# A shifted copy in DRAM: two free-running DMA queues, or one queue in turns with waits

## The chip, the cores and the metric

The kernel runs on one core of a Trainium2 chip. The metric is the device time of one execution in microseconds; the time of a kernel is the median over its runs. The profiles show one execution each.

## The reference

```python
def setup_inputs():
    return {"x": np.random.randn(8192, 8192).astype(np.float32)}

def reference(x):
    return np.fft.ifftshift(x)
```

For an even size in both dimensions this swaps the four quadrants: `out[r, c] = x[(r + 4096) % 8192, (c + 4096) % 8192]`. Nothing is computed; 268.44 MB are read and as many written. A half row, 4096 float32 or 16 KB, is the longest run that is contiguous in both `x` and `out`. Rows lie 32 KB apart.

## The kernel before

All work is DMA from DRAM to DRAM; SBUF isn't used. `copy(queue, row, h, step)` issues one transfer (L29) of 256 half rows, 4 MB: output rows `row` to `row + 255`, left half (`h = 0`) or right half (`h = hc`). Its access pattern has the outer dimension `[C, ENGINES]`: 16 rows that follow each other, one for each of the core's 16 DMA engines. The middle one, `[step * C, per]` with a step of 16, gives an engine 16 rows, each 16 rows on from the one before. So in a transfer the sixteen engines go side by side through adjacent rows. A half row is one packet.

The loop (L36 to L39) takes 1024 rows at a time in four blocks of 256. The sync queue (engine SP, DMA queue q1 in the profile) copies the left halves of the blocks in order, the scalar queue (ACT, q10) the right halves, two blocks off. That makes 32 transfers on each queue. The kernel writes no waits itself; the framework that orders the program adds them. At the start each queue issues four transfers; each later one waits for the transfer four before it on its queue. So up to eight transfers (32 MB) are in flight. At the end of the program (L65) SP waits for what has not landed. L54 belongs to the program's setup.

Of the kernel before, what the change touches and what calls it, by code (L numbers as in the profile page):

```python
# [1 line left out]

# [4 lines left out]


ENGINES = 16


@with_exitstack
def kernel(
    ctx: ExitStack,
    tc: tile.TileContext,
    x: bass.AP,
    out: bass.AP,
):
    nc = tc.nc
    R, C = x.shape  # L20
    hr = R // 2
    hc = C // 2
    per = 16
    rows = ENGINES * per

    def copy(queue, row, h, step):

        dims = [[C, ENGINES], [step * C, per], [1, hc]]
        queue.dma_start(  # L29
            out=bass.AP(out.tensor, out.offset + row * C + h, dims),  # L30
            in_=bass.AP(x.tensor, x.offset + (row + hr) % R * C + hc - h, dims),
        )

    for first in range(0, R, 4 * rows):  # L36
        for n in range(4):
            copy(nc.sync, first + n * rows, 0, ENGINES)
            copy(nc.scalar, first + (n + 2) % 4 * rows, hc, ENGINES)  # L39


# [1 line left out]
_INS = ['x']  # L43
_OUTS = [((8192, 8192), 'float32')]


def kernel(**inputs):
    import numpy as _np
    import concourse.bacc as _bacc
    import concourse.tile as _tile  # L50
    from concourse import mybir as _mybir
    from concourse.bass_utils import run_bass_kernel_spmd as _run

    nc = _bacc.Bacc("TRN2", target_bir_lowering=False, num_devices=1)  # L54
    arrays, args = {}, []
    for name in _INS:
        a = _np.ascontiguousarray(inputs[name])
        if a.dtype.kind in "iu":
            a = a.astype(_np.int64)
        arrays[f"in_{name}_dram"] = a  # L60
        args.append(nc.dram_tensor(f"in_{name}_dram", a.shape, _mybir.dt.from_np(a.dtype), kind="ExternalInput").ap())
    for i, (shape, dtype) in enumerate(_OUTS):
        dt = _mybir.dt.from_np(_np.dtype(dtype))
        args.append(nc.dram_tensor(f"out_{i}_dram", shape, dt, kind="ExternalOutput").ap())
    with _tile.TileContext(nc) as tc:  # L65
        kernel(tc, *args)
    r = _run(nc, [arrays], core_ids=[0])
    got = tuple(r.results[0][f"out_{i}_dram"] for i in range(len(_OUTS)))
    return got[0]
```

## Time and profile before

| | |
|---|---|
| median of 2 runs | 823.39 us (820.27 to 826.52) |
| span of the profiled execution | 812.4 us |
| recorded times less this span | 7.9 and 14.1 us, 11.0 at the median |
| data moved | 268.44 MB read, 268.44 MB written |
| share of the 16 DMA engines' span | q1 49.7%, q10 49.5% |
| transfers | 32 by SP, 32 by ACT, 4096 KB each |
| from issue to landing, median | 101.0 us |

The span is from the first to the last instruction on the core; the time of a run also holds what lies around it. The profile names a DMA queue's share as the time that its packets took, over the span of sixteen engines: shares that add up to 100% mean that no engine was without a packet. In a table of stretches each row has the stretch, its length, the busy time of GpSimd (only the setup), the granted clock, the DMA share and GB/s.

### The profile page before, as it was taken

How to read it: one execution, taken by the hardware profiler on the slowest of the kernel's cores; microseconds unless marked ns; L12 is line 12 of the kernel's file. 1: busy time of each engine (PE TensorE's matmuls, PEld its weight loads, DVE VectorE, ACT ScalarE, POOL GpSimd, SP SyncE). 2: the span in 40 equal slices, each digit the busy share in tenths (PEclk: the TensorE clock that was granted, in tenths of full speed). 3: DMA queues.
4: the chain of work that ended last, by engine and by line, in shares of the span. 5: the costliest groups of instructions: out<-in, count | busy, mean ns of one | idle time of the engine just before them, and what ended most of it. 6: DMA issues, size and time to landing. Idle time of an engine off the chain costs nothing. (4 is left out here: it accounts for less than half of the span.)

```text
span 812.4 us, 109 instructions
## 1 busy us (share of the span) xinstructions
POOL 0.2 (0%) x4
## 2 busy tenths in 40 slices
POOL 0000000000000000000000000000000000000000
DMA  9999999999999999999999999999999999999998
GB/s 307 331 331 336 335 331 331 335 325 337 334 332 336 331 333 332 334 339 332 332 334 331 329 331 334 332 328 333 330 334 335 334 328 333 332 331 330 338 331 280
DMA packets 17408, 268.44 MB, mean 330 GB/s; under 512 B 1024, under 2 KB 1024, under 8 KB 1024
## 3 DMA queue, kind: packets, MB, share of 16 engines
q1 hardware_dynamic: 8704, 134.22, 49.7%
q10 hardware_dynamic: 8704, 134.22, 49.5%
HBM read 268.44 MB, written 268.44 MB: 661 GB/s over the span
## 5 line engine op out<-in xcount | busy, mean ns | idle before, releaser
L54 POOL MEMSET const-bfloat16-1.0<- 128x1 bf16 x1 | 0.1, 101 | 0.0
L54 POOL MEMSET const-uint8-127<- 128x1 uint8 x1 | 0.1, 101 | 0.0
L54 POOL MEMSET const-float32-0.0<- 128x1 f32 x1 | 0.1, 98 | 0.2 <-issue 0.2
L54 POOL MEMSET const-float32-1.0<- 128x1 f32 x1 | 0.1, 98 | 0.0
## 6 DMA issues: line engine op xcount, KB each, us to landing
out_dram<-in_x_dram SPq DMA_DIRECT2D x32, 4096.0 KB, 101.0
out_dram<-in_x_dram ACTq DMA_DIRECT2D x32, 4096.0 KB, 101.0
```

What stands on the lines that cost most here:

```text
L54: nc = _bacc.Bacc("TRN2", target_bir_lowering=False, num_devices=1)
```

## The change

The ACT queue is no longer used. `copy` gets the number of half rows per engine and a semaphore, and its pattern is one dimension of `16 * per` rows in place of two. The 8192 rows are cut into eight parts of 1024. Each part has its own turn size (half rows per engine in a turn) and rest. A turn copies `16 * turn` rows, first all the left halves, then in a turn of its own all the right halves. Part 0 issues its eight transfers of 4 MB at once. In the other parts a turn is two transfers: the main one, of `turn - rest` half rows per engine, and behind it the rest. Before the main one SP waits until all main transfers so far have landed; rests are not waited for until the end. The block is kept in the order written, with its own two semaphores.

```diff
-    per = 16
-    rows = ENGINES * per
 
-    def copy(queue, row, h, step):
+    def copy(queue, row, h, per, sem):
 
-        dims = [[C, ENGINES], [step * C, per], [1, hc]]
+        dims = [[C, ENGINES * per], [1, hc]]
+        dst = out.offset + row * C + h
+        src = x.offset + (row + hr) % R * C + hc - h
         queue.dma_start(
-            out=bass.AP(out.tensor, out.offset + row * C + h, dims),
-            in_=bass.AP(x.tensor, x.offset + (row + hr) % R * C + hc - h, dims),
-        )
+            out=bass.AP(out.tensor, dst, dims),
+            in_=bass.AP(x.tensor, src, dims),
+        ).then_inc(sem, ENGINES)
 
+    part = 1024
+    plan = ((16, 0), (16, 1), (16, 2), (16, 3), (16, 4), (32, 2), (32, 3), (8, 2))
 
-    for first in range(0, R, 4 * rows):
-        for n in range(4):
-            copy(nc.sync, first + n * rows, 0, ENGINES)
-            copy(nc.scalar, first + (n + 2) % 4 * rows, hc, ENGINES)
+    with tc.tile_critical(), nc.semaphore("main") as main, nc.semaphore("end") as end:
+        mains = ends = 0
+        for k, (turn, rest) in enumerate(plan):
+            rows = ENGINES * turn
+            for first in range(k * part, (k + 1) * part, rows):
+                for h in (0, hc):
+                    if rest:
+                        nc.sync.wait_ge(main, mains)
+                    copy(nc.sync, first, h, turn - rest, main)
+                    mains += ENGINES
+                    if rest:
+                        copy(nc.sync, first + ENGINES * (turn - rest), h, rest, end)
+                        ends += ENGINES
+        nc.sync.wait_ge(main, mains)
+        nc.sync.wait_ge(end, ends)
```

The program before issues 32 transfers on SP and 32 on ACT; the changed one issues 120 on SP (8 in part 0, 112 in the others) and none on ACT. 56 turns begin with a wait.

## The prediction

> **What bounds the kernel now.** I read the page's head and its DMA section first: no compute engine works, and the sixteen DMA engines are full.
>
> ```profile
> span 812.4 us, 109 instructions
> ...
> DMA packets 17408, 268.44 MB, mean 330 GB/s; under 512 B 1024, under 2 KB 1024, under 8 KB 1024
> ## 3 DMA queue, kind: packets, MB, share of 16 engines
> q1 hardware_dynamic: 8704, 134.22, 49.7%
> q10 hardware_dynamic: 8704, 134.22, 49.5%
> HBM read 268.44 MB, written 268.44 MB: 661 GB/s over the span
> ```
>
> The two queues' packets (q1 is fed by SP, q10 by ACT) took 99.2% of sixteen engines' span. So the time is set by how long a packet of 16 KB, one half row, occupies an engine. 16384 of the packets carry data, 1024 for each engine.
>
> Next I read the DMA view of the middle alone, 10 to 800 us, to have a steady rate without the two ends.
>
> ```profile
> DMA packets 17017, 262.56 MB, mean 332 GB/s; under 512 B 992, under 2 KB 992, under 8 KB 992
> ```
>
> 262.56 MB in 790 us is 332.4 GB/s, or 20.8 GB/s for each engine: one half row per engine every 0.79 us. All 268.44 MB at this rate are 807.7 us.
>
> Then the stretches around the start and the end, and the waits of SP, because the change makes many small starts and ends out of one of each.
>
> ```profile
> 0.00:2.10 2.10, 0.20 (x4) 1.00 0.00 0
> 2.10:2.30 0.20, 0.00 (x0) 1.00 3.31 819
> ...
> 2.00:3.00 1.00, 0.00 (x0) 1.00 1.05 262
> 3.00:6.00 3.00, 0.00 (x0) 1.00 1.04 404
> 6.00:9.00 3.00, 0.00 (x0) 1.00 1.00 350
> 9.00:12.00 3.00, 0.00 (x0) 1.00 0.99 328
> 12.00:15.00 3.00, 0.00 (x0) 1.00 0.98 300
> ...
> 806.00:808.00 2.00, 0.00 (x0) 1.00 0.96 328
> 808.00:810.00 2.00, 0.00 (x0) 1.00 0.54 180
> 810.00:813.00 3.00, 0.00 (x0) 1.00 0.01 5
> ```
>
> The last column is GB/s, the one before it the DMA share; a packet's bytes count where it starts.
>
> ```profile
> L29 SPq DMA_DIRECT2D out_dram<-in_x_dram x32: 571/571/652, 0.7 to 708.6; - x32
> ...
> DMA to landing us min/median/max: 25.6/101.0/103.4
> ...
> SPq L29 <- DMA out_dram<-in_x_dram: 689.4, 28, 25.3
> SPq L65 <- DMA out_dram<-in_x_dram: 102.2, 2, 79.5
> ```
>
> SP issues first at 0.73 (timeline), and the first packets start at about 2.1: 1.4 us from an issue to bytes. SP's last issue ends at 708.6 + 0.57 = 709.2, and its last wait ends 102.2 us later, at 811.4: the last landing. SP does wait 28 times already (L29), but for the oldest of eight transfers in flight, with about 100 us of work queued behind it. Those waits cost no DMA time: the share is 1.00 from 20 us on.
>
> **The change, part by part.**
>
> *Same work.* The bytes, the 16 KB packets and their number per engine stay: 1024 x 0.79 us, 807.7 us in all, if the rate stays. Semaphore packets grow from 64 to 120 for each engine; the 64 of before lie inside a share of 99 to 100% and show no gap, so I cost the other 56 at nothing.
>
> *ACT's issues move to SP.* SP issues 120 transfers instead of 32. At 0.57 us that is 68 us of an otherwise waiting SP, spread over more than 800. The second issue of a turn (the rest) runs while the engines work on the first, so it is free. Only the 0.57 us of the first issue after a wait is exposed, and that is inside the 1.4 us above. A transfer of 480 rows in place of 256 may take longer to issue: between nothing and another 0.57 us; I take nothing, from the flat 571 ns of the shape seen.
>
> *The waits.* This is the term that counts. Up to part 0 there is no wait. From part 1 on each of the turns (8 each in parts 1 to 4, 4 each in parts 5 and 6, 16 in part 7) starts with a wait until every engine has landed the main share of the turn before: 56 waits. Behind the waiting instruction on SP stand the turn's main issue, its rest and all later turns; nothing else feeds the engines. So while the slowest engine ends, the semaphore travels and the new issue takes effect, the engines have only the rest of the turn before: 1 to 4 half rows each.
>
> What a wait costs with no rest at all, the one start and the one end of this profile tell together. From the first issue to the last landing are 811.4 - 0.7 = 810.7 us, at the steady rate the bytes need 807.7. So one run-down and one restart cost 3.0 us: 1.4 of the restart and 1.6 of engines that run out one after another (180 and 5 GB/s in the last rows) and of landing, less what the quick first microseconds give back. I take the 1.4 whole. The 1.6 comes after 810 us in which the engines could drift apart; after a turn of 6 to 25 us they should be closer, so I take three quarters, 1.2: 2.6 us for a bare wait. Its bounds are 3.0 (all of it) and 1.4 (no drift, landing for nothing). A rest of R covers R x 0.79 us.
>
> The cover of a wait is the rest of the turn before, so a part's first wait has the rest of the part before it. Counted from the plan: 1 wait with no rest, 8 with a rest of 1, 27 with 2, 12 with 3, 8 with 4.
> - rest 0: 2.6 x 1 = 2.6
> - rest 1: (2.6 - 0.79) x 8 = 14.5
> - rest 2: (2.6 - 1.58) x 27 = 27.5
> - rest 3: (2.6 - 2.37) x 12 = 2.8
> - rest 4: covered, 0
>
> Sum 47.4 us. With 3.0 for a bare wait it is 3.0 + 17.7 + 38.3 + 7.6 = 66.6; with 1.4 it is 1.4 + 4.9 = 6.3. If the longer issue is exposed too, 56 x 0.57 = 32 us come on top.
>
> *The layout.* Before, the sixteen engines copy sixteen adjacent rows at a time (outer dimension ENGINES, step ENGINES inside). Now one dimension of 16 x per rows is handed out; if each engine gets a run of it, engines stand 6 to 31 rows (192 to 992 KB) apart, and all work on the same half. No row shows this layout. The bounds I take are the slowest and quickest stretches of the start: 300 GB/s (12 to 15 us) and 404 (3 to 6 us). I take the steady 332, since q1 and q10 hold opposite halves and no slice of the page's middle leaves 325 to 339 whatever their mix.
>
> The Trainium skill's page "DMA: Bandwidth & Descriptors", section "Latency and other measured facts", speaks against a layout of far rows: copies between HBM tensors ran at 207 GB/s with a pitch of 512 KiB and at 214 with the pitch padded. No run here shows it yet. Taken for all parts, 807.7 x 214 / 207 would be 27 us more, an estimate from that page.
>
> *Sum.* Span 812.4 + 47.4 = 859.8 us. The two recorded times are 820.27 and 826.52, median 823.39, so 11.0 us lie around the span at the median. Forecast 870.8, say 871 us: 5.8% slower.
>
> **The rivals.**
>
> *Lockstep pays (faster).* A common start seems to run better: 404 GB/s at 3 to 6 us, 350 at 6 to 9, against 332. Each wait that lets engines idle starts them together again, and the 7/8 of the bytes in parts 1 to 7 (234.9 MB, 706.7 us) could run at the rate of a fresh start. From 2 to 9 us 2.52 MB started, 361 GB/s: 234.9 MB then take 651 us, 56 less, which with 47 of waits gives 823 - 9 = 814. At 404 throughout it is 581 us, 125 less: 745. It decides above 356 GB/s, where 234.9 MB take 47 us less; it counts as faster from 365. For it: the start is no single packet, but 6 us. Against it: 9 to 15 us ran at 328 and 300, below the mean, so the lead was given back within a turn; the first rows count sixteen packets that had only started; and rests of 3 and 4 leave no idle time in which engines could line up. "HBM Reference" of the Trainium skill, section "Specifications (TRN2)", gives about 716 GB/s for a domain, 358 each way for a copy; by it the time would not fall below 823 - 51 + 47 = 819. The trace's 661 read and written agrees; its 404 each way in three microseconds does not.
>
> *The rest hides the wait.* If engines stay within a packet of each other and landing is quick, only rests of 0 and 1 leave a gap: 6.3 us, 830 us, within 2%. For it: 1.4 us of restart is less than two packets. Against it: the end needs more than 2 us to run down.
>
> *The layout is worse.* At the 300 GB/s of the slowest stretch 268.44 MB take 895 us, 87 more: 958 with the waits. For it: nothing but the distance of the rows and the same half on all engines. Against it: the steady rate under any mix.
>
> **How the numbers follow.** My forecast has 0.5: 835 to 920 (6.3 plus some landing at the low end, 98 us of waits and longer issues at the high one). Lockstep 0.2, of which 0.15 ends more than 2% faster and 0.05 about even; the hidden wait 0.13; the worse layout 0.17, at 900 to 960. About 2% is what a measurement of this kernel can tell from no change. So faster 0.16, same 0.18, slower 0.66. The range that holds 8 in 10 leaves out the far lockstep and the far layout: 790 to 925.
>
> **What would show it.** In the profile after, the DMA share of the stretches: 1.00 in part 0 (to about 100 us), some 0.87 in part 1 (rest 1, 1.8 us of 12.6 + 1.8 idle), 0.92 in part 2, 0.98 in part 3, 1.00 in part 4, 0.96 in part 5, 0.99 in part 6 and 0.86 in part 7 (1.0 us of 6.3 + 1.0), and the mean of a busy engine unchanged, so that GB/s falls as the share. SP's waits on the copy's line should be 56 beside the last ones. I am wrong if the share falls but the GB/s does not (lockstep), if the share stays at 1.00 in part 1 (the wait is hidden), or if the GB/s in part 0, where nothing waits, is already off 332 (layout or the single queue).

## The result, and the profile after

The changed kernel takes 878.62 us (878.32 to 878.92, two runs) against 823.39 us: 1.0667 times as long, 95% interval 1.0594 to 1.0741. The forecast was 871.

The head of the page after, with its only working queue:

```profile
span 877.1 us, 168 instructions
...
DMA packets 18305, 268.45 MB, mean 306 GB/s; under 512 B 1920, under 2 KB 1920, under 8 KB 1920
...
q1 hardware_dynamic: 18304, 268.44, 92.1%
...
HBM read 268.44 MB, written 268.44 MB: 612 GB/s over the span
```

Where 99.2% of the engines' span were packets, it is 92.1% now. These 7.1% of 877 us are 62 us more than before in which engines have nothing to do.

The same by stretches, one for each part of the plan (DMA share and GB/s last):

```profile
2.00:108.00 106.00, 0.00 (x0) 1.00 0.98 317
108.00:223.00 115.00, 0.00 (x0) 1.00 0.88 292
223.00:333.00 110.00, 0.00 (x0) 1.00 0.92 305
333.00:441.00 108.00, 0.00 (x0) 1.00 0.94 308
441.00:548.00 107.00, 0.00 (x0) 1.00 0.94 313
548.00:658.00 110.00, 0.00 (x0) 1.00 0.94 309
658.00:763.00 105.00, 0.00 (x0) 1.00 0.97 318
763.00:875.00 112.00, 0.00 (x0) 1.00 0.84 302
```

Share and rate don't move alike. Part 7 has the lowest share, 0.84, and yet moves 302 GB/s, more than part 1 with 0.88 and 292. Part 0, which has no wait, has 317 and is below the 332 GB/s of before.

The start of the changed kernel, and SP's waits:

```profile
2.00:3.00 1.00, 0.00 (x0) 1.00 0.82 262
3.00:6.00 3.00, 0.00 (x0) 1.00 0.98 371
6.00:9.00 3.00, 0.00 (x0) 1.00 1.02 333
9.00:12.00 3.00, 0.00 (x0) 1.00 0.96 289
12.00:15.00 3.00, 0.00 (x0) 1.00 0.97 289
```

```profile
SPq L34 <- DMA out_dram<-in_x_dram: 766.4, 56, 71.5
SPq L56 <- DMA out_dram<-in_x_dram: 6.9, 1, 6.9
```

The 56 waits are there. The quick start of before (404, then 350) comes again weaker and ends in 289 GB/s.

How long an engine stood idle around a wait can be read from the packets' own starts and ends in the trace: the engines without a packet (16 less the packets under way; the trace doesn't name a packet's engine), from 3 us before SP's main issue to 6 us after it, summed and divided by 16.

| part | turn, rest | idle per wait, forecast | measured | DMA share, forecast | measured |
|---|---|---|---|---|---|
| 1 | 16, 1 | 1.81 us | 1.86 us | 0.87 | 0.88 |
| 2 | 16, 2 | 1.02 | 1.20 | 0.92 | 0.92 |
| 3 | 16, 3 | 0.23 | 0.87 | 0.98 | 0.94 |
| 4 | 16, 4 | 0 | 0.87 | 1.00 | 0.94 |
| 5 | 32, 2 | 1.02 | 1.24 | 0.96 | 0.94 |
| 6 | 32, 3 | 0.23 | 1.10 | 0.99 | 0.97 |
| 7 | 8, 2 | 1.02 | 1.15 | 0.86 | 0.84 |

Times the waits (8, 8, 8, 8, 4, 4, 16) that is 66 us of idle engines, where 47 were forecast.

The rows of the table are means of a part, and a part's first wait is covered by the rest of the part before it. Sorted by the rest that really lay behind a wait, the idle agrees better with the forecast for short rests and worse for long ones:

| rest behind the wait | waits | idle per wait, forecast | measured | sum, forecast | measured |
|---|---|---|---|---|---|
| 0 | 1 | 2.6 us | 2.49 us | 2.6 us | 2.5 us |
| 1 | 8 | 1.81 | 1.80 | 14.5 | 14.4 |
| 2 | 27 | 1.02 | 1.22 | 27.5 | 32.9 |
| 3 | 12 | 0.23 | 0.81 | 2.8 | 9.8 |
| 4 | 8 | 0 | 0.85 | 0 | 6.8 |

The 27 waits with a rest of 2 fall apart by the length of the turn before them: 1.07 us after turns of 16, 1.15 after turns of 8, 1.76 after turns of 32. The means of the longer rests hold a few long waits: one in part 3 has 2.61 us, the other seven of that part 0.36 to 0.95.

### The profile page after: what moved, and what is told of

Same layout as the page of the kernel before. It is cut to its first block, busy times and chain, and to the rows that moved or that the text cites. A ratio compares the mean times of both kernels' runs of the same rounds, so it can differ in the third digit from the quotient of the medians.

```text
span 877.1 us, 168 instructions
## 1 busy us (share of the span) xinstructions
POOL 0.2 (0%) x4
## 3 DMA queue, kind: packets, MB, share of 16 engines
q1 hardware_dynamic: 18304, 268.44, 92.1%
## 6 DMA issues: line engine op xcount, KB each, us to landing
out_dram<-in_x_dram SPq DMA_DIRECT2D x8, 3840.0 KB, 14.4
out_dram<-in_x_dram SPq DMA_DIRECT2D x8, 3072.0 KB, 13.2
```

## The experiments

Chips differ, so each kernel is compared with the kernel before on the same chip: 823.91 us for the first four kernels, 821.99 for the next four, 813.49 for three of the last group and 823.96 for the kernel with a rest of 5. Ratios are what is compared.

**Is the copy itself slower? Four kernels.** The first keeps the changed `copy` and its one queue but has no wait until the end:

```diff
-    plan = ((16, 0), (16, 1), (16, 2), (16, 3), (16, 4), (32, 2), (32, 3), (8, 2))
+    plan = ((16, 0),) * 8
```

(In the diffs that follow, "..." stands for lines that aren't shown, the old plan among them.)

> All eight parts as part 0 of the change: one queue, blocks of rows per engine, no wait until the end. Theory Base (the copy itself became slower: part 0 ran at 316 GB/s against 332 before): 268.44 MB at 316 GB/s are 849 us, with the ends and the time around the span about 861 us; packets of about 812 ns, DMA share near 0.98. Theory Waits (only the 56 waits cost, part 0 is a start effect): at 332 GB/s, 821 to 827 us.

828.78 us, ratio 1.0061 (1.0043 to 1.0080). Theory Base falls: not 37 us but 5 belong to the copy. Its stretches show how 317 GB/s in part 0 and this fit together:

```profile
2.00:100.00 98.00, 0.00 (x0) 1.00 1.00 318
100.00:200.00 100.00, 0.00 (x0) 1.00 0.99 322
200.00:300.00 100.00, 0.00 (x0) 1.00 1.00 326
...
400.00:500.00 100.00, 0.00 (x0) 1.00 1.00 329
...
700.00:800.00 100.00, 0.00 (x0) 1.00 1.00 330
```

The share is full from the start, but the packets are slower at first: a single queue begins at 318 GB/s and comes up to 330 over some 400 to 600 us. Without a wait SP still can't issue everything at once: the first five issues of this run take 0.6 to 0.7 us each, the median of all 64 is 12.0. In part 0 of the change, too, the last three of the eight issues hold SP for 7.2, 13.2 and 11.9 us.

The second adds the pattern of before to that:

```diff
...
-        dims = [[C, ENGINES * per], [1, hc]]
+        dims = [[C, ENGINES], [ENGINES * C, per], [1, hc]]
```

> As the run without waits, but with the pattern of before (sixteen adjacent rows side by side): only the queue and the order differ from before. If the loss of the base rate is the layout: about 823 us. If it is the single queue (or the same half on all engines): the same time as the run without waits, about 861 us by theory Base. By theory Waits 823 us in any case.

825.44 us, 1.0028 (1.0004 to 1.0051), with the same slow start (318, then 324 GB/s). So the slow start isn't the layout.

The third is the kernel before with the changed pattern:

```diff
-        dims = [[C, ENGINES], [step * C, per], [1, hc]]
+        dims = [[C, ENGINES * per], [1, hc]]
```

> The kernel before with its two queues and order, only the pattern changed to one dimension of 256 rows. If the layout costs the base rate: about 861 us. If the single queue does: 823 us. By theory Waits 823 us.

822.58 us, 0.9984 (0.9966 to 1.0002). Two queues run at 330 GB/s in the first 100 us, in the changed layout too:

```profile
2.00:100.00 98.00, 0.00 (x0) 1.00 1.00 330
100.00:200.00 100.00, 0.00 (x0) 1.00 1.00 330
```

Without waits the changed pattern costs nothing. The slow start goes with the single queue, or with what comes with it: all engines work on the same half. No run here separates these two.

The fourth keeps all turns and waits of the change and takes the pattern of before (the same two lines as in the second):

> The change with all its turns and waits, but the pattern of before in every transfer. If the layout costs the base rate, 37 us come back: about 841 us. If the single queue does, or by theory Waits, the time of the change stays, 878 us. If engines that start together gain from adjacent rows (404 GB/s at 3 to 6 us of before, 371 of the change), parts 1 and 7, which restart from idle, gain beyond the others.

892.58 us, 1.0848 (1.0821 to 1.0874): none of the expectations. With waits, adjacent rows are slower than the change (1.0594 to 1.0741), where without waits they were not. The idle per wait is about that of the change (1.84, 1.22, 0.94, 1.15, 1.43, 1.16, 1.16 us in parts 1 to 7), 70 us in all. By the packets' own times, this kernel loses 14 us against the change: 4 of idle, and 9 because a packet takes 797 ns in the mean, where it takes 788 in the change. Without waits the two patterns are at 797 and 800 ns. So the waits shorten the packets of the change in the mean, and not those of this kernel (one trace each). Why stays open.

**Is it the waits, and what do they cost? Four kernels.** The first leaves everything in the change as it is, but lets a wait look at the main transfer before the last, with one semaphore for even and one for odd turns:

```diff
...
-                        nc.sync.wait_ge(main, mains)
-                    copy(nc.sync, first, h, turn - rest, main)
-                    mains += ENGINES
+                        nc.sync.wait_ge(mains[n % 2], counts[n % 2])
+                    copy(nc.sync, first, h, turn - rest, mains[n % 2])
+                    counts[n % 2] += ENGINES
+                    n += 1
...
```

> The change with its plan, turns, rests and 120 transfers as they are; only what a wait waits for is moved: the main transfer before the last one, on a semaphore of its own in turn, so a full turn lies behind every wait. If the time went into idle engines at the waits: about 829 us, as without waits. If it went into the smaller transfers, their issues or the order of the rows: the 878 us of the change stay.

826.91 us, 1.0065 (1.0040 to 1.0090), the same as without waits. The waits are still there, the idle is not:

```profile
SPq L34 <- DMA out_dram<-in_x_dram: 706.9, 56, 59.3
```

```profile
100.00:200.00 100.00, 0.00 (x0) 1.00 1.00 321
200.00:300.00 100.00, 0.00 (x0) 1.00 1.00 328
...
700.00:800.00 100.00, 0.00 (x0) 1.00 1.00 328
```

SP waits as many times and nearly as long (706.9 against 766.4 us). So the 120 smaller transfers, their issues and the order of the rows cost nothing that shows beside a run without waits, and the time of the change above 1.006 is the idle at the waits.

The second has turns of 16 with a wait and nothing behind it:

```diff
...
+    plan = ((16, 0),) * 8
...
-                    if rest:
+                    if mains:
                         nc.sync.wait_ge(main, mains)
```

> Turns of 16 with no rest at all, and a wait before each: 63 bare waits. Theory Linear (the prediction: a bare wait costs 2.6 us and a rest of R takes 0.79 R off): 829 us of the run without waits + 63 x 2.6 = 993 us. Theory Skew (a wait costs restart plus landing plus how far the engines stand apart, and a larger rest lets them stand farther apart): bare waits bring the engines together each time, the least skew of all; idle of 1.86 us seen with a rest of 1, plus the 0.79 us of the missing rest, 2.65 us: about the same 990 us. Both fall if it is under 950 or over 1030 us.

978.54 us, 1.1912 (1.1868 to 1.1955). Above a run without waits (1.006 x 822 = 827) these are 151 us, 2.40 us for each of 63 waits; idle by the packets is 2.45. The forecast bare wait of 2.6 us was near. With rests of 0, 1 and 2 behind turns of 16 the idle is 2.45, 1.80 and 1.07 us, some 0.7 us less for each row where 0.79 were forecast.

```profile
100.00:900.00 800.00, 0.00 (x0) 1.00 0.84 275
```

The third covers a wait with eight rows:

```diff
...
+    plan = ((16, 8),) * 8
```

> All turns 16 with a rest of 8: 6.3 us of cover behind each of 64 waits. Theory Linear: no cost from a rest of 4 on, 829 us as without waits. Theory Skew: a rest of 4 still left 0.87 us idle per turn because the engines stood up to 3 us apart; 6.3 us cover that too, 829 to 835 us. If a floor of about 0.87 us a wait stays whatever the cover (something in the wait itself, not the distance of the engines): 829 + 64 x 0.87 = 885 us.

827.70 us, 1.0060 (1.0033 to 1.0088), idle 0.08 us a wait. A wait has no price of its own; enough work behind it hides it whole:

```profile
SPq L34 <- DMA out_dram<-in_x_dram: 732.2, 63, 13.0
```

```profile
400.00:500.00 100.00, 0.00 (x0) 1.00 1.00 328
```

The fourth runs part 7 throughout:

```diff
...
+    plan = ((8, 2),) * 8
```

> All parts as part 7 (turns of 8, rest of 2): 128 waits. By the time of part 7 in the change, 112.7 us, eight such parts: 902 us. Theory Linear, priced at 1.02 us a wait on top of the run without waits: 829 + 128 x 1.02 = 960 us. The difference would be the quick microseconds after a restart, which a short turn has nearly all the time (packets of 729 ns in part 7 against 784 to 812 in the others).

896.31 us, 1.0911 (1.0862 to 1.0959). The idle is 1.03 us a wait, 131 us in all over 127 waits, but the time above 827 is only 69. Half of the idle comes back. In the turns of 16 without rest none did (154 us idle, 151 lost). The stretch without the two ends has nearly the share of the bare waits, and a tenth more GB/s:

```profile
100.00:800.00 700.00, 0.00 (x0) 1.00 0.86 302
```

The difference is what the engines do after a restart. Counting bytes evenly over each packet, the microseconds from 1.5 after the issue on move 250, 367, 408, 359 and 373 GB/s here, mean 351, and then the engines run out of the turn. In the bare turns of 16 they move 253, 385, 420, 342, 340, 333, 330, 317, 310, 303, 294 and 301, mean 327: the lead is given back in the second half of the turn.

**Where does cover end? Three more runs, and one try for a faster order.** All turns as part 4:

```diff
...
+    plan = ((16, 4),) * 8
```

> All parts as part 4 of the change (turns of 16, rest of 4): 64 waits with 3.2 us of cover. Theory Linear: 829 us, as without waits. Theory Skew: the 0.87 us idle per turn seen in part 4 comes again in every turn, because 3.2 us do not cover restart, landing and engines that stand 2 to 3 us apart: 8 x 106.6 us of part 4 = 853 us, at most 829 + 64 x 0.87 = 885 us.

Its four runs took 904 to 948 us, where before took 813.49 on that chip; they spread too far for a ratio, but the quickest is still 11% above before. No theory expected that; part 4 of the change was far better. The profiled run, 920.8 us, is not the quickest, so it shows how the time is lost and not the least that is lost:

```profile
200.00:300.00 100.00, 0.00 (x0) 1.00 0.82 274
...
600.00:700.00 100.00, 0.00 (x0) 1.00 0.95 321
```

In 30 of its 63 turns with a wait exactly one packet was under way when SP issued: a single engine still had its rest to do. It ended the rest at 2.06 to 2.74 us after the issue (2.08 mostly: its main share ended 0.36 us before the issue, and four packets of 0.61 follow). Fifteen engines had new packets mostly at 1.3 to 1.7 us; in most of these turns the packets under way came back to sixteen only at about 3.4. So the late engine began a turn 2 us after the others, the others waited for the end of its main share, and these turns idle 2.0 to 3.4 us, where the mean of all 63 waits is 1.88. That it is the same engine from turn to turn is likely and not shown, since the trace doesn't name engines. In part 1 of the change (rest 1) the last engine is through 0.2 to 0.4 us after the issue, before the new transfer comes, and sixteen packets start together; in part 2 (rest 2) it is through at 0.3 to 1.3 us. With a rest of 4, the rest that should cover the wait delayed the one engine that all waited for. The long wait of 2.61 us in part 3 of the change looks the same: one packet under way at the issue.

One row more:

```diff
...
+    plan = ((16, 5),) * 8
```

> All turns 16 with a rest of 5, one more than in the run that took 904 to 948 us. In that run's packets one engine was last in turn after turn: it ended its rest 2.08 us after SP's next issue and took up the new transfer only at about 3.4, while the fifteen others had done so at 1.3 to 1.7. Theory Late engine: what makes a long rest harmful is that the last engine's own rest delays it, and then a fixed pause of about 1.3 us follows: it ends at 2.7 and takes up the new transfer at 4.0; the turns stay long, 880 to 950 us. Theory Fetch: the new transfer is ready for a busy engine about 3.4 us after the issue whatever it does; with a rest of 5 the pause shrinks to 0.7 us and the time to some 850 to 880 us. Theory Linear: no cost, as with a rest of 8: 1.006 of before, 820 to 830 us by the chip.

842.74 us, 1.0258 (1.0210 to 1.0305), between the expectations of Linear and Fetch; Late engine falls, at least on this chip. The share is 0.95 to 0.99:

```profile
100.00:200.00 100.00, 0.00 (x0) 1.00 0.97 316
...
400.00:500.00 100.00, 0.00 (x0) 1.00 0.95 320
```

No turn had the single late engine. What was left is 0.40 us of idle a wait. About half of it is engines that run out before the new packets come, some 1.3 us after the issue, most of all in 11 waits of 0.75 us and more; the rest is mostly one or two engines idle from 1.5 to 3 us. So the cover is whole somewhere between 5 and 8 rows, not at 3.3 (2.6 / 0.79) as forecast. Why the late engine kept itself alive in the one run and not in the other, and whether that depends on the chip, stays open.

A single queue without waits, whose engines are set apart at the start by transfers that use the lower engines alone:

```diff
...
+                    if not mains:
+                        row = 0
+                        for n in (8, 4, 2, 2):
+                            copy(nc.sync, row, h, 0, main, n)
+                            mains += ENGINES
+                            row += n
+                        copy(nc.sync, row, h, turn - 1, main)
...
```

> The run without waits, but the first sixteen half rows go as transfers of 8, 4, 2 and 2 rows, which use the lower engines alone: engines 0 to 7 start with one to four half rows more, so the engines stand up to 3 us apart from the start instead of after 700 us. If a single queue is slow at first (316 GB/s in the first 100 us, 330 at the end) because its engines are in step: about 330 GB/s from the start, less the 3 us at the end that the uneven load costs, 820 to 825 us. If it is something else that settles with time: 316 GB/s at first again, 830 to 833 us.

817.25 us, 1.0068 (1.0034 to 1.0101) on the chip where before took 813.49. The stretches from the start are 324, 330 and 333 GB/s, with 333 at the end: the queue settles in 200 us instead of some 400. That speaks for engines in step as the cause of the slow start, but the first stretch is still 3% low, the time against before did not improve on the run without waits (1.0061), and the chip was another. It is not settled.

The try:

```diff
-    for first in range(0, R, 4 * rows):
-        for n in range(4):
-            copy(nc.sync, first + n * rows, 0, ENGINES)
-            copy(nc.scalar, first + (n + 2) % 4 * rows, hc, ENGINES)
+    for first in range(0, hr, rows):
+        for h in (0, hc):
+            copy(nc.sync, first, h, ENGINES)
+            copy(nc.scalar, hr + first, hc - h, ENGINES)
```

(with the pattern of one dimension.)

> Two queues as before, blocks per engine, no own waits; SP copies the upper 4096 rows and ACT the lower, each on opposite halves, so the two queues are never in the same rows. A try for a faster order. Theory Same (the memory's rate doesn't depend on which rows the queues are in): 823 us. If near rows of the two queues disturb each other: faster than 815 us. If far ones do: slower than 832 us.

813.32 us, 1.0015 (0.9986 to 1.0044): the same. No run here beat the kernel before.

## Why the prediction came out right, and where its steps did not

*The level.* The sum started from the profiled span, 812.4 us, and put 11.0 us "around the span". In every run since, time and span differ by 1.8 us (829.18 and 827.4 in the run without waits). The 11.0 were mostly another thing: the profiled execution of before was some 9 us quicker than the recorded ones. Chips differ as much: before took 813.49 us on one of them. The term did its work, the level of the recorded runs, under a wrong name.

*The waits.* The mechanism was right: with the same transfers and a wait one turn back the loss is gone. In time the waits cost 1.0667 less 1.006, some 50 us (44 to 56 by the interval of the change), where 47.4 were forecast. That the two are so near is in part luck, since errors of opposite sign met in that sum:
- Long rests were mis-sized. Bare waits and rests of 1 came as forecast, but the 20 waits covered by 3 or 4 rows were priced at 2.8 us together and are 16.6 by the packets, and the 27 waits covered by 2 are 32.9 where 27.5 were priced, more than half of the excess after the turns of 32. The idle is 66 us in place of 47. The cover R x 0.79 assumed that a row of rest takes a full 0.79 us and that the distance of the engines stays the same. A packet takes 0.61 us where few engines are at work. And the engines spread with longer rests: from first to last, the sixteen landings of a main transfer lie about 1.0 us apart in part 1 and 1.3 to 2.9 us in part 4. That the longer rest causes the spread is argued, by the late engine, and not shown by a run of its own.
- The waits were priced at their idle time, and part of that comes back as shorter packets: 788 ns in the mean against 800 without waits, which over 1024 packets for each engine is 12 us. Most of it lies in part 7, with packets of 729 ns where those of parts 1 to 6 take 784 to 801.

The term for a longer issue was rightly put at nothing: the main issues behind a wait take 0.51 us for 480 rows as for 96.

*The copy.* "The rate stays" was off by a little: one queue without waits costs 1.006, 5 us. The step that put part 0 at a share of 1.00 and 332 GB/s read the steady rate of two queues as that of any queue. Part 0 at 317 GB/s is one of the signs that the prediction named for being wrong (332 missed where nothing waits), and part 7, where the share falls and the rate falls less, is in part another (lockstep). Both showed, and both are small beside the waits.

*The rivals.* Lockstep pays: in a turn of 16 without rest no, in a turn of 8 by half of what it costs. The first rows of before already held the answer, 404 and 350 followed by 328 and 300; what the forecast left out is that a turn of 8 ends before the payback. The hidden wait: 2 rows don't hide it and 5 not quite; 8 do. The worse layout: no loss without waits, for the two kernels without waits differ by 0.3%, and the adjacent one is on the quick side by less than 4 us. Which rows an engine gets, no trace shows; by the plan the distance of a main transfer's engines would be 6 to 30 rows, not 31.

The Trainium skill's page "DMA: Bandwidth & Descriptors", section "Latency and other measured facts", has 207 GB/s for a pitch of 512 KiB and 214 as the full rate, the latter with a pitch of 4 MiB padded by 4 KiB; by an estimate from it the far rows would have cost 27 us, if that rule held between engines. No such loss shows here, and both kernels without waits run at 318 to 330 GB/s.

## What to carry to other kernels

A full wait on a stream of transfers can be priced from the one start and the one end that the profile already holds: 3.0 us there, 2.4 us measured. The 3.0 is a small difference of two spans over 800 us, so take it as a rough size. To hide the wait, put more behind it than restart and landing together: here 3 or 4 rows of 0.79 us were meant to suffice and left 0.8 us a wait, 8 left 0.08. A rest that is too short can even hurt, where the slowest engine still has its own rest to do when the next transfer is issued. Waiting for the transfer before the last is simpler and cost nothing here beyond the run without waits. Read rates after a restart over the whole turn: the first five microseconds had 351 GB/s here, the first twelve 327.
